# The first two pairs' modulation fetched pair by pair, and three small loads written later

## The chip, the cores and the metric

The kernel runs on one core of one Trainium2 chip. The metric is the device time of one execution in microseconds (us). A core has five engines, each with its own in-order instruction queue, that meet only at semaphores: TensorE (PE in the profile, its weight loads PEld), VectorE (DVE), ScalarE (ACT), GpSimd (POOL) and SyncE (SP). In this kernel SP does nothing but issue DMAs. Sixteen DMA engines move what SP and POOL issue.

## The reference

One layer over 256 latent tokens `x` and 256 context tokens `ctx`, width 2048, all in float32. Only the beginning matters here:

```python
mod_x = (silu(c)     @ w_mod + b_mod).reshape(1, 1, 9, 2048)   # w_mod: 2048 x 18432
mod_c = (silu(c_ctx) @ w_mod + b_mod).reshape(1, 1, 9, 2048)
# first half-step feed-forward, the same for x (mod_x) and ctx (mod_c):
h = rms_norm(x, norm_ffn1) * (1 + mod[1]) + mod[0]
x = x + 0.5 * mod[2] * ((silu(h @ w_gate) * (h @ w_up)) @ w_down)   # 2048 -> 5504 -> 2048
# then: mixer (gated heads | two-direction scan), second feed-forward, final norm
```

So the first feed-forward can't start before parts 0 and 1 of `w_mod` (2 x 2048 columns, 33.5 MB) have been read, multiplied and applied, at least for the input channels it starts with. The scan heads have three small parameter rows, `dt_bias`, `a_log` and `d_skip`, used much later.

## The kernel before, in words

The 2048 channels are 16 tiles of 128, taken as eight **pairs** (kp = 0 to 7). Both token sets stand side by side, 512 columns. Every product is done in three matmuls (`mm3`, L116 to L118): each float32 operand is cut into a high part `hi` (ACT, L68) and a rest `lo` (DVE, L69), and hi*hi, hi*lo and lo*hi are added up.

Start: SP loads x and ctx (tiles `xin`), PE transposes them (L296), ACT squares them, DVE and POOL add the squares up. `rstd_rows` makes the row norm from that: `total` (16 small matmuls, L272), `root` (DVE, ACT, DVE up to `dg`), `spread` (a matmul, L283, and the ACT copy `R`).

Modulation of pairs (`first_mods`, L529): `w_mod` comes in 512 KB tiles `raw`, which are multiplied on PE with silu(c) (`sc`). Eight tiles make up one pair's share of parts 0 and 1, sixteen that of two pairs. A **half** is the work on two tiles: four matmuls of 512 columns, or eight of 256. With `cnt` = 2, two pairs are done together, first all of part 1, then all of part 0, from tiles of 128 x 2 x 512, so with rows of 2 KB in memory. With `cnt` = 1, one pair has both parts in one bank, from tiles of 128 x 4 x 256, rows of 1 KB. After the last half of a bank DVE copies it out (`m`, L373), PE turns it (L378), DVE reduces it and adds the bias (L381, L386), and `scale_of` (L393) makes the scale from part 1. `first_h(kp)` then makes the pair's input: DVE multiplies by the row norm (`xr`, L324), ACT applies scale and shift (`hh` and `t`, L332), DVE takes the rest (`hl`, L337).

First feed-forward columns (`first_cols`): for each pair, gate and up weights of 3 x 128 columns (two tiles of 384 KB, called g0, u0 for pair 0 and so on), 36 matmuls of 512 columns for each pair, into six banks. This is a loop over pairs, 288 matmuls in all, and between them the halves of later pairs are woven in at numbered places (`weave`, the table `between`; a place is one mm3, and pair kp begins at place 12*kp). After it come five chunks of the feed-forward, whose weights no longer need a modulation first.

Order: each engine's queue is fixed when the program is built. A scheduler places the instructions by priorities of its own; the order in which the code is written, and the places of `weave`, steer it, and only the pinned instructions (`keep_in_program_order`) keep their written order. SP's queue is in order too, so a load that waits for a buffer holds up all loads behind it. All weight tiles share one pool of seven buffers `raw` (`rp`, bufs=7); a tile is loaded once its buffer's former tile has been used: by PE for `w_mod`, by ACT and DVE for weights that are cut into hi and lo. The cut halves share three buffers each.

Of the kernel before, what the change touches and what calls it, by code (L numbers as in the profile page):

```python
# [15 lines left out]
P = 128  # L16
# [18 lines left out]
def tile_block(ctx: ExitStack, tc: tile.TileContext, a, out: bass.AP):  # L35
# [18 lines left out]
    def const(shape, n, dt=F32):  # L54
        return cp.tile(shape, dt, tag=n, name=n)

    def small(t, src):
        nc.gpsimd.dma_start(t, src)

    def raw(shape, src):  # L60
        t = rp.tile(shape, F32, tag="raw", name=uid("raw"))
        nc.sync.dma_start(t, src)
        return t
# [14 lines left out]
    def loaded(shape, src):  # L78
        return lambda: split(raw(shape, src), shape)
# [29 lines left out]
    def mbank():  # L109
        return mp.tile([P, 512], F32, tag="mi", name=uid("mi"))  # L110
# [18 lines left out]


    bias_bc = const([P, 32], "bias_bc")
    small(bias_bc, a["dt_bias"].rearrange("o d h -> o (d h)").partition_broadcast(P))
    alog_bc = const([P, 32], "alog_bc")
    small(alog_bc, a["a_log"].rearrange("o d h -> o (d h)").partition_broadcast(P))
    dsk = const([P, NH], "dsk")
    small(dsk, a["d_skip"].partition_broadcast(P))


    cv = const([P, 2, KT], "cv")
# [65 lines left out]
    def then(f):  # L205
        tasks[-1][2].append(f)
# [42 lines left out]
    def xcol(k, v):  # L249
        return xpair(k // 2, v)[:, k % 2, :]  # L250
# [116 lines left out]
    def mod_take(ps, parts):  # L367

        st = {}

        def copy():
            st["m"] = slot([P, 512], n="m")
            tc.keep_in_program_order(nc.vector.tensor_copy(st["m"], ps))  # L373

        def turn():
            pt = mbank()
            for i in range(4):
                nc.tensor.transpose(pt[:, i * P:(i + 1) * P], st["m"][:, i * P:(i + 1) * P], ident)  # L378
            for i, (part, tp) in enumerate(parts):
                dst = MOD[part][:, 2 * tp:2 * tp + 2, :]  # L380
                nc.vector.tensor_reduce(  # L381
                    out=dst,
                    in_=pt[:, i * 256:(i + 1) * 256].rearrange("p (t g w) -> p t w g", g=4, w=32)[:, :, 0:2, :],
                    axis=mybir.AxisListType.X, op=ALU.add,
                )
                tt(dst, dst, bmod(part, 2 * tp, 2).unsqueeze(2).broadcast_to([P, 2, 2]), op=ALU.add)  # L386

        return copy, turn

    def scale_of(part, n, k0=0, k1=KT):  # L390

        m = MOD[part][:, k0:k1, :]
        stt(m, m, 1.0, vec(n, k0, k1 - k0).unsqueeze(2).broadcast_to([P, k1 - k0, m.shape[2]]),  # L393
            op0=ALU.add, op1=ALU.mult)

    def column(part):
        return lambda k, v: MOD[part][:, k, v:v + 1]
# [99 lines left out]
    def first_mods(k0, cnt):  # L497


        steps, turns = [], []  # L500

        def bank_of(parts):
            st = {}

            def half(i, j0):

                w = []
                part, kp = parts[i]
                n0 = part * D + kp * 256

                def load():
                    for x in range(2):
                        if cnt == 2:
                            w.append(raw([P, 2, 512], wmod[:, j0 + 2 * x:j0 + 2 * x + 2, n0:n0 + 512]))
                        else:
                            w.append(raw([P, 4, 256], wmod[:, j0 + 4 * x:j0 + 4 * x + 4, n0:n0 + 256]))

                first, last = ((0, 1, 2, 3), (12, 13, 14, 15)) if cnt == 2 else ((4, 5, 6, 7), (8, 9, 10, 11))

                def run_():  # L520
                    if not st:
                        st["ps"] = mbank()
                        st["take"] = mod_take(st["ps"], parts)

                    for y in ((2, 3, 0, 1) if cnt == 2 else (4, 5, 6, 7, 0, 1, 2, 3)):
                        j, g = j0 + y, y % 4
                        o, src = (st["ps"], w[y // 2][:, y % 2, :]) if cnt == 2 else (
                            st["ps"][:, i * 256:(i + 1) * 256], w[y // 4][:, g, :])
                        tc.keep_in_program_order(nc.tensor.matmul(  # L529
                            o[32 * g:32 * g + 32, :], lhsT=sc[:, j, :], rhs=src, start=(j == first[g]), stop=(j == last[g])))  # L530

                return load, run_

            if cnt == 2:
                steps.extend(half(0, j0) for j0 in range(0, KT, 4))
            else:
                steps.extend(half(i, j0) for i in range(2) for j0 in range(0, KT, 8))
            steps.append((None, lambda: st["take"][0]()))
            turns.append(lambda: st["take"][1]())

        if cnt == 2:
            for part in (1, 0):
                bank_of(((part, k0), (part, k0 + 1)))
        else:
            bank_of(((1, k0), (0, k0)))
        turns.append(lambda: scale_of(1, "norm_ffn1", 2 * k0, 2 * (k0 + cnt)))
        return steps, turns
# [3 lines left out]
    def first_h(kp):  # L551
        for _, f in modulated(kp, (0, 1), lambda v: R0["R"][:, v * TX:(v + 1) * TX], column(1), column(0)):
            f()

    m0, t0 = first_mods(0, 2)
    for load, _ in m0:
        if load:
            load()
    total, root, spread = [f for _, f in pieces]
    for f in (*[f for _, f in m0[:5]], total, small_turn, root, *[f for _, f in m0[5:7]], t0[0], spread,  # L560
              *[f for _, f in m0[7:]], *t0[1:], lambda: first_h(0)):
        f()

    between = {1: [lambda: first_h(1)]}
    later = []

    def place(at, f):
        between.setdefault(at, []).append(f)  # L570

    def weave(k0, cnt, at):
        steps, turns = first_mods(k0, cnt)
        for (load, f), x in zip(steps, at):
            if load:
                later.append(load)
            place(x, f)
            if load:
                place(x, ahead)
        place(at[len(steps)], lambda: [t() for t in turns])  # L580
        place(at[len(steps)], lambda: first_h(k0))
        if cnt == 2:
            place(12 * k0 + 1, lambda: first_h(k0 + 1))
# [2 lines left out]
        if later:  # L586
            later.pop(0)()

    weave(2, 2, [1, 3, 5, 7, 8, 9, 11, 13, 15, 16, 17])
    weave(4, 2, [19, 21, 24, 26, 27, 29, 32, 34, 37, 38, 39])  # L590
    weave(6, 1, [42, 46, 50, 54, 55, 56])
    weave(7, 1, [58, 62, 66, 70, 71, 73])

    g0 = []

# [53 lines left out]
    def down(m0, n, act_t, vs, after=lambda dg: None, steps=1, budget=0.0):  # L649
        a0, a1 = vs[0] * TX, (vs[-1] + 1) * TX  # L650

        def fold(d, ps):
            while len(gates_done) <= d // 8:
                next(bg)
            for v in vs:
                x = xcol(d, v)
                stt(x, ps[:, v * TX:(v + 1) * TX], MOD[2][:, d, v:v + 1], x, op0=ALU.mult, op1=ALU.add)

        def unit(dg, st, f0, fn):
            def mm(hl_):  # L660
                hi, lo = hl_
                if f0 == 0:
                    st.extend([(dbank if dg % 2 else bank)() for _ in range(2)])
                for dd in range(2):
                    c = slice(dd * P, (dd + 1) * P)
                    for i in range(fn):
                        f = f0 + i
                        h, l = act_t[f]
                        mm3(st[dd][:, a0:a1], (hi[:, i, c], lo[:, i, c]), (h[:, a0:a1], l[:, a0:a1]), f == 0, f == n - 1)

            add(loaded([P, fn, 256], krows(wd, m0 + f0, fn, dg * 256, 256)), mm, steps, budget)

        for dg in range(KP):
            st = []
            for f0 in range(0, n, 4):
                unit(dg, st, f0, min(4, n - f0))
            for dd in range(2):
                then(lambda dg=dg, dd=dd, st=st: fold(2 * dg + dd, st[dd]))
            then(lambda dg=dg: after(dg))
# [22 lines left out]
    for ci, n in enumerate(chunks):  # L702
        m0 = m
        act_t = []
        if m == 0:
            for t in range(N0):
                then(lambda t=t, dst=act_t: gated(dst, g0[t], g0[N0 + t]))
            m = N0
        while m < m0 + n:
            pair(m, act_t, 1.5 if ci == 0 else 1.2)  # L710
            m += 2
        if ci < len(chunks) - 1:
            down(m0, n, act_t, (0, 1), steps=0.9 if ci == 0 else 0.7)
    then(lambda: [None for _ in bg])
    then(root_table)
    for v in range(2):
# [694 lines left out]
    t0 = len(tasks) - 8  # L1411
# [108 lines left out]
```

## Time and profile before

| | |
|---|---|
| median of 3 runs | 2655.83 us (2655.7 to 2657.45) |
| the profiled execution | 2657.01 us, its span 2655.3 us |
| PE busy | 2616.2 us, 99% of the span |
| DVE, ACT, POOL busy | 1617.7, 979.6, 56.2 us |
| HBM read | 492.77 MB, 186 GB/s over the span |

The profile is one execution on the chip. Busy time is given by engine and by stretch of time; a wait is put down to the instruction or DMA whose semaphore came last. The granted clock is the share of TensorE's full speed; 1.00 is the level of 2.4 GHz and 0.50 that of 1.2 GHz, and a stretch with both has a value in between.

### The profile page before, as it was taken

To read this page: it belongs to the slowest core of one execution; us is meant where nothing else is said; L and a number is where in the kernel's file an instruction comes from. 1 tells how busy PE (TensorE), PEld (TensorE's weight loads), DVE (VectorE), ACT (ScalarE), POOL (GpSimd) and SP (SyncE) were. 2 spreads that over 40 slices of the span, in tenths; PEclk is the share of its full clock that TensorE was granted. 3 is DMA by queue.
4 is the path that set the end of the run, shared out by engine and by line. 5 is a ranking of instruction groups with operands and counts; after the bars stand their busy time and mean duration, and the time that the engine had idled before them with its cause. 6 is when DMAs were issued, how large, how long until landed. Compare 5 with 4: busy or idle time off the path is not lost.

```text
span 2655.3 us, 31810 instructions
## 1 busy us (share of the span) xinstructions
PE 2616.2 (99%) x12309; PEld 2132.3 (80%) x12309; DVE 1617.7 (61%) x2167; ACT 979.6 (37%) x1326; POOL 56.2 (2%) x84
## 2 busy tenths in 40 slices
PE   6999999999999999999999999999999999999998
PEld 3577888888888888888889977778788888888896
DVE  3378987876555556556324855876654445455646
ACT  4342222212222222222223654765564443434344
POOL 2000000000000000000000000021010000000000
PEclk8999999999999999999999999999999999999999
DMA  9976766657665766766434543355666666666664
GB/s 314 317 240 201 224 211 203 195 172 211 203 194 164 217 189 207 220 190 205 119 102 132 175 131 88 111 173 164 199 199 189 192 189 194 188 195 186 196 179 139
DMA packets 333547, 499.06 MB, mean 188 GB/s; under 512 B 18835, under 2 KB 169683, under 8 KB 333395
## 3 DMA queue, kind: packets, MB, share of 16 engines
q1 hardware_dynamic: 331059, 491.21, 60.0%
q0 software_dynamic: 2336, 5.81, 0.9%
q8 instruction: 96, 1.57, 0.2%
q14 instruction: 56, 0.46, 0.0%
HBM read 492.77 MB, written 2.10 MB: 186 GB/s over the span
## 4 chain that ended last, share of the span: by engine, by line
PE 95%; DMA 2%; DVE 1%; ACT 1%; issue 0%; SPq 0%; ACTq 0%; DVEq 0%
PE gu L116 25%; PE gu L117 25%; PE gu L118 25%; PE dn L116 5%; PE dn L117 5%; PE dn L118 5%; PE mi L529 1%; DMA raw<-in_w_mod_dram 1%; PE dn L982 0%; DVE cy L903 0%; PE mi L411 0%; PE mi L1356 0%; PE mi L1052 0%; PE mi L1081 0%; ACT hi L68 0%
## 5 line engine op out<-in xcount | busy, mean ns | idle before, releaser
L69 DVE TENSOR_TENSOR lo<-raw,hi 128x1024 fp32r<-128x1024 f32 (+1 forms) x634 | 759.9, 1199 | 777.8 <-ACT hi L68 777.0
L68 ACT CAST hi<-raw 128x1024 fp32r<-128x1024 f32 (+1 forms) x634 | 650.1, 1026 | 1446.0 <-PE gu L117 755.5
L116 PE MATMUL gu<-hh,hi 128*128 128x512 f32 x1504 | 590.0, 393 | 1.9 <-ACT hh L332 1.6
L118 PE MATMUL gu<-hh,lo 128*128 128x512 f32 x1504 | 587.2, 390 | 0.0
L117 PE MATMUL gu<-hl,hi 128*128 128x512 f32 x1504 | 587.1, 390 | 0.0
L459 DVE SCALAR_TENSOR_TENSOR macc<-raw,sc,macc 128x512 f32<-128x512 f32 x600 | 424.5, 746 | 4.9
L116 PEld LDWEIGHTS gu<-hh,hi 128*128 128x128 f32 x1504 | 283.0, 188 | 75.5 <-issue 7.2
L116 PE MATMUL gu<-hi,hh 128*128 128x512 f32 (+1 forms) x864 | 336.3, 390 | 0.0
L117 PE MATMUL gu<-lo,hh 128*128 128x512 f32 (+1 forms) x864 | 334.3, 387 | 0.0
L118 PE MATMUL gu<-hi,hl 128*128 128x512 f32 (+1 forms) x864 | 333.6, 386 | 0.0
L117 PEld LDWEIGHTS gu<-hl,hi 128*128 128x128 f32 x1504 | 282.9, 188 | 61.2 <-issue 4.3
L118 PEld LDWEIGHTS gu<-hh,lo 128*128 128x128 f32 x1504 | 282.6, 188 | 61.3 <-issue 2.2
L116 PEld LDWEIGHTS gu<-hi,hh 128*128 128x128 f32 x864 | 162.3, 188 | 32.0 <-issue 1.4
L117 PEld LDWEIGHTS gu<-lo,hh 128*128 128x128 f32 x864 | 162.3, 188 | 31.8 <-issue 1.4
L118 PEld LDWEIGHTS gu<-hi,hl 128*128 128x128 f32 x864 | 162.2, 188 | 31.8 <-issue 0.7
L116 PE MATMUL gu<-ah,hi 128*128 128x512 f32 (+1 forms) x408 | 145.6, 357 | 0.0
L116 PE MATMUL dn<-ah,hi 128*128 128x512 f32 (+1 forms) x408 | 145.4, 356 | 0.0
L118 PE MATMUL dn<-ah,lo 128*128 128x512 f32 (+1 forms) x408 | 145.4, 356 | 0.0
L117 PE MATMUL dn<-al,hi 128*128 128x512 f32 (+1 forms) x408 | 145.2, 356 | 0.0
L117 PE MATMUL gu<-al,hi 128*128 128x512 f32 (+1 forms) x408 | 145.2, 356 | 0.0
L118 PE MATMUL gu<-ah,lo 128*128 128x512 f32 (+1 forms) x408 | 145.1, 356 | 0.0
L116 PEld LDWEIGHTS dn<-ah,hi 128*128 128x128 f32 x408 | 77.1, 189 | 12.6 <-ACT hi L68 0.8
(309 smaller groups left out, 2549.4 us busy)
## 6 DMA issues: line engine op xcount, KB each, us to landing
raw<-in_w_mod_dram SPq DMA_DIRECT2D x288, 512.0 KB, 4.7
raw<-in_ffn_w_down_dram SPq DMA_DIRECT2D x172, 512.0 KB, 3.9
raw<-in_ffn_w_gate_dram SPq DMA_DIRECT2D x160, 512.0 KB, 4.4
raw<-in_ffn_w_up_dram SPq DMA_DIRECT2D x160, 512.0 KB, 4.2
raw<-in_w_in_dram SPq DMA_DIRECT2D x72, 512.0 KB, 3.7
raw<-in_w_out_dram SPq DMA_DIRECT2D x32, 512.0 KB, 3.8
raw<-in_ffn_w_gate_dram SPq DMA_DIRECT2D x16, 384.0 KB, 4.0
raw<-in_ffn_w_up_dram SPq DMA_DIRECT2D x16, 384.0 KB, 3.4
```

Source lines behind the costliest of these rows:

```text
L68: a = nc.scalar.copy(hi, src)
L69: b = nc.vector.tensor_tensor(lo, src, hi.bitcast(F32), op=ALU.subtract)
L116: nc.tensor.matmul(ps, lhsT=wh, rhs=xh, start=first, stop=False)
L117: nc.tensor.matmul(ps, lhsT=wh, rhs=xl, start=False, stop=False)
L118: nc.tensor.matmul(ps, lhsT=wl, rhs=xh, start=False, stop=last)
L459: tc.keep_in_program_order(stt(acc[v], w[:, i, :], s, acc[v], op0=ALU.mult, op1=ALU.add))
L529: tc.keep_in_program_order(nc.tensor.matmul(o[32 * g:32 * g + 32, :], lhsT=sc[:, j, :], rhs=src, start=(j == first[g]), stop=(j == last[g])))
```

## The change

The first two pairs are no longer done together. Pair 0 alone is fetched and done ahead of the column loop (eight tiles of 128 x 4 x 256 in place of sixteen of 128 x 2 x 512). Pair 1 is woven into pair 0's columns (`weave(1, 1, ...)`), and the places of the later pairs are moved. In the start, `small_turn`, `total` and `root` are written among the four halves of pair 0, and the turn after the copy. The three loads of the heads' parameters are written behind the second feed-forward chunk.

```diff
-    small(bias_bc, a["dt_bias"]...)      # and a_log, d_skip
+    def head_parameters():
+        small(bias_bc, a["dt_bias"]...)  # and a_log, d_skip
...
-    m0, t0 = first_mods(0, 2)
+    m0, t0 = first_mods(0, 1)
...
-    for f in (*[f for _, f in m0[:5]], total, small_turn, root, *[f for _, f in m0[5:7]], t0[0], spread,
-              *[f for _, f in m0[7:]], *t0[1:], lambda: first_h(0)):
+    for f in (*[f for _, f in m0[:2]], total, small_turn, root, m0[2][1], spread, m0[3][1], m0[4][1], *t0, lambda: first_h(0)):
...
-    between = {1: [lambda: first_h(1)]}
+    between = {}
...
-    weave(2, 2, [1, 3, 5, 7, 8, 9, 11, 13, 15, 16, 17])
-    weave(4, 2, [19, 21, 24, 26, 27, 29, 32, 34, 37, 38, 39])
+    weave(1, 1, [1, 3, 5, 7, 8, 10])
+    weave(2, 2, [9, 11, 12, 13, 14, 15, 16, 17, 18, 19, 22])
+    weave(4, 2, [24, 26, 28, 30, 31, 32, 34, 36, 38, 39, 42])
...
+        if ci == 1:
+            then(head_parameters)
```

From the end of the first columns on, every engine's queue is the same as before. Up to there the same instructions stand in another order, with four more small ones on DVE. On POOL the scheduler puts the three loads at the start again, only behind the first masks instead of ahead of `ident`.

**First place, VectorE (DVE) at the step from pair 0 to pair 1.** Before, pair 1's scale and shift came with pair 0's, and its `xr` and `hl` follow pair 0's; `lo_180` is u1's rest, and `m_183` the first copy of pairs 2 and 3:

```order
L337 TENSOR_TENSOR hl_73_323<-t_133_476,hh_72_322 128x512
L324 TENSOR_TENSOR xr_167_544<-xt_23_151,R_127_445 128x512
L69 TENSOR_TENSOR lo_154_517<-raw_152_514,hi_153_516 128x768
L324 TENSOR_TENSOR xr_168_546<-xc_31_159,R_127_445 128x512
L337 TENSOR_TENSOR hl_75_325<-t_169_548,hh_74_324 128x512
L337 TENSOR_TENSOR hl_77_327<-t_170_553,hh_76_326 128x512
L69 TENSOR_TENSOR lo_180_600<-raw_178_597,hi_179_599 128x768
L373 COPY m_183_620<-mi_171_560 128x512
```

Now, with `lo_165` as u1's rest and `m_168` as the copy of pair 1's modulation:

```order
L339 TENSOR_TENSOR hl_73_320<-t_122_445,hh_72_319 128x512
L69 TENSOR_TENSOR lo_165_565<-raw_163_562,hi_164_564 128x768
L375 COPY m_168_589<-mi_156_513 128x512
L326 TENSOR_TENSOR xr_173_616<-xt_23_148,R_116_414 128x512
L326 TENSOR_TENSOR xr_174_618<-xc_31_156,R_116_414 128x512
L383 TENSOR_REDUCE mod1_308<-mi_172_606 128x4
```

The copy that pair 1's input hangs on now stands behind the rest of u1, a tile that before pair 1's input did not wait for.

**Second place, SyncE (SP) ahead of pair 2.** The `raw` tiles in the order of their issue. Before, from u1 (`raw_178`) to g2 (`raw_189`), the tile whose rest DVE takes ahead of the last copy for pairs 2 and 3:

```order
L62 DMA raw_178_597<-in_ffn1_w_up_dram 128x2x384
L62 DMA raw_181_613<-in_w_mod_dram 128x2x512
L62 DMA raw_182_615<-in_w_mod_dram 128x2x512
L62 DMA raw_185_630<-in_w_mod_dram 128x2x512
L62 DMA raw_186_632<-in_w_mod_dram 128x2x512
L62 DMA raw_187_644<-in_w_mod_dram 128x2x512
L62 DMA raw_188_646<-in_w_mod_dram 128x2x512
L62 DMA raw_189_648<-in_ffn1_w_gate_dram 128x2x384
```

Now, from g2 (`raw_179`) to u2 (`raw_194`); here it is u2 whose rest (`lo_196`) DVE takes ahead of the last copy (`m_199`):

```order
L62 DMA raw_179_643<-in_ffn1_w_gate_dram 128x2x384
L62 DMA raw_182_656<-in_w_mod_dram 128x2x512
L62 DMA raw_183_658<-in_w_mod_dram 128x2x512
L62 DMA raw_184_667<-in_w_mod_dram 128x2x512
L62 DMA raw_185_669<-in_w_mod_dram 128x2x512
L62 DMA raw_188_684<-in_w_mod_dram 128x2x512
L62 DMA raw_189_686<-in_w_mod_dram 128x2x512
L62 DMA raw_190_695<-in_w_mod_dram 128x2x512
L62 DMA raw_191_697<-in_w_mod_dram 128x2x512
L62 DMA raw_192_706<-in_w_mod_dram 128x2x512
L62 DMA raw_193_708<-in_w_mod_dram 128x2x512
L62 DMA raw_194_710<-in_ffn1_w_up_dram 128x2x384
```

By the semaphores in the built programs g2 took the buffer of u1 before (free when DVE has cut u1), and u2 now takes the buffer of `raw_184` (free when PE has run the seventh half of pairs 2 and 3, `raw_185` and `raw_184`).

**Third place, TensorE (PE) at the step from pair 1 to pair 2.** Before, from the eighth half of pairs 2 and 3 over the last turn to pair 2's first matmul:

```order
L529 MATMUL mi_184_625<-raw_186_632,sc_135 32x512 x2
L529 MATMUL mi_184_625<-raw_185_630,sc_135 32x512 x2
L378 MATMUL mi_198_699<-ident_128,m_196_685 128x128 x4
L529 MATMUL mi_206_737<-raw_188_646,sc_135 32x512 x2
L529 MATMUL mi_206_737<-raw_187_644,sc_135 32x512 x2
L529 MATMUL mi_206_737<-raw_193_666,sc_135 32x512 x2
L529 MATMUL mi_206_737<-raw_192_664,sc_135 32x512 x2
L116 MATMUL gu_155_520<-hh_78_328,hi_190_650 128x512
```

Now, from the seventh half on:

```order
L531 MATMUL mi_187_679<-raw_185_669,sc_132 32x512 x2
L531 MATMUL mi_187_679<-raw_184_667,sc_132 32x512 x2
L117 MATMUL dn_148_493<-hl_77_324,hi_164_564 128x512
L118 MATMUL dn_148_493<-hh_76_323,lo_165_565 128x512
L380 MATMUL mi_200_741<-ident_125,m_186_674 128x128 x4
L116 MATMUL dn_149_494<-hh_76_323,hi_164_564 128x512
L117 MATMUL dn_149_494<-hl_77_324,hi_164_564 128x512
L118 MATMUL dn_149_494<-hh_76_323,lo_165_565 128x512
L531 MATMUL mi_187_679<-raw_189_686,sc_132 32x512 x2
L531 MATMUL mi_187_679<-raw_188_684,sc_132 32x512 x2
L380 MATMUL mi_201_750<-ident_125,m_199_730 128x128 x4
L116 MATMUL gu_144_489<-hh_78_325,hi_180_645 128x512
```

Before, two halves of pairs 4 and 5 stand between the last turn and pair 2's first matmul; now nothing does.

## Rows read from the trace of the kernel before

**Rows 1.** Stretches: length, busy us of five engines, granted clock, DMA share, GB/s.
```profile
83.29:152.50 69.21, 64.94 (x389) 42.41 (x386) 30.15 (x57) 33.67 (x58) 0.00 (x0) 0.97 0.92 309
21.00:42.00 21.00, 15.70 (x89) 5.13 (x89) 7.38 (x19) 6.77 (x11) 4.78 (x4) 0.76 1.05 389
118.50:128.00 9.50, 9.50 (x62) 6.82 (x51) 3.67 (x5) 4.90 (x9) 0.00 (x0) 1.00 1.08 357
```

**Rows 2.** Timeline of PE ahead of the columns: start, us, instruction [idle before <-releaser].
```profile
24.63 1.93 PE L529 MATMUL mi<-raw,sc 128*32 128x512 f32 x8 [1.57 <-DMA raw<-in_w_mod_dram]
...
33.96 1.95 PE L272 MATMUL dn<-ones,sq 128*128 128x1 f32 x16
...
37.41 1.12 PE L283 MATMUL dn<-dg,ones 128*128 128x512 f32 x2
...
43.56 1.94 PE L529 MATMUL mi<-raw,sc 128*32 128x512 f32 x8 [1.66 <-DMA raw<-in_w_mod_dram]
...
49.03 2.07 PE L116 MATMUL gu<-hh,hi 128*128 128x512 f32 x4 [1.59 <-ACT hh L332]
```

**Rows 3.** Timeline of PE in the columns: halves, two matmuls, turns.
```profile
53.59 1.15 PE L529 MATMUL mi<-raw,sc 128*32 128x512 f32 x8
...
67.83 0.39 PE L117 MATMUL gu<-hl,hi 128*128 128x512 f32 x1
68.06 0.39 PE L118 MATMUL gu<-hh,lo 128*128 128x512 f32 x1
...
79.80 0.66 PE L378 MATMUL mi<-ident,m 128*128 128x128 f32 x4 [2.02 <-DVE m L373]
80.39 2.97 PE L529 MATMUL mi<-raw,sc 128*32 128x512 f32 x16
83.29 1.52 PE L116 MATMUL gu<-hh,hi 128*128 128x512 f32 x3
...
131.97 1.93 PE L529 MATMUL mi<-raw,sc 128*32 128x256 f32 x32
```

**Rows 4.** Timeline of ACT: cut of u1; cut of g2, input of pair 2; the same of pair 6.
```profile
67.89 0.83 ACT L68 CAST hi<-raw 128x768 fp32r<-128x768 f32 x1 [10.06 <-DMA raw<-in_ffn_w_up_dram]
77.32 0.83 ACT L68 CAST hi<-raw 128x768 fp32r<-128x768 f32 x1 [8.60 <-DMA raw<-in_ffn_w_gate_dram]
81.26 1.09 ACT L332 ACTIVATE hh<-xr,mod,mod 128x256 fp32r<-128x256 f32 x2 [3.11 <-DVE mod L386]
...
128.90 0.83 ACT L68 CAST hi<-raw 128x768 fp32r<-128x768 f32 x1 [3.23 <-DMA raw<-in_ffn_w_up_dram]
133.04 1.09 ACT L332 ACTIVATE hh<-xr,mod,mod 128x256 fp32r<-128x256 f32 x2 [3.31 <-DVE mod L393]
```

**Rows 5.** Timeline of DVE: rest of g2 and the copy behind it; the copy for pair 6.
```profile
78.19 0.96 DVE L69 TENSOR_TENSOR lo<-raw,hi 128x768 fp32r<-128x768 f32 x1 [4.18 <-ACT hi L68]
79.06 0.68 DVE L373 COPY m<-mi 128x512 f32<-128x512 f32 x1
...
130.64 0.68 DVE L373 COPY m<-mi 128x512 f32<-128x512 f32 x1
```

**Rows 6.** Timeline of SP: issue of u1 and of g2.
```profile
61.07 0.42 SPq L62 DMA_DIRECT2D raw<-in_ffn_w_up_dram  x1
...
71.83 0.42 SPq L62 DMA_DIRECT2D raw<-in_ffn_w_gate_dram  x1
```

**Rows 7.** The page, DMA issues: count, KB each, median us from issue to landing.
```profile
raw<-in_ffn_w_up_dram SPq DMA_DIRECT2D x16, 384.0 KB, 3.4
```

**Rows 8.** Timeline of ACT at the start: `a_log`'s exponential, the first square.
```profile
7.61 0.23 ACT L831 ACTIVATE alog_bc<-alog_bc 128x32 f32<-128x32 f32 x1 [5.52 <-DMA alog_bc<-in_a_log_dram]
...
9.87 0.63 ACT L301 ACTIVATE sq<-xt 128x512 f32<-128x512 f32 x1 [0.47 <-DVE xt L299]
```

**Rows 9.** Timeline of POOL at the start: first and last instruction now ahead of the loads.
```profile
3.07 0.22 POOL masks.py:197 MEMSET ident<- 128x128 f32 x1
...
4.42 0.29 POOL L181 TENSOR_SCALAR_AFFINE_SELECT GE<-ones 128x128 f32<-128x128 f32 x1
```

More of the change, by code (lines that the diff above doesn't have):

```diff
@@ L131, in tile_block @@
     bias_bc = const([P, 32], "bias_bc")
-    small(bias_bc, a["dt_bias"].rearrange("o d h -> o (d h)").partition_broadcast(P))
     alog_bc = const([P, 32], "alog_bc")
-    small(alog_bc, a["a_log"].rearrange("o d h -> o (d h)").partition_broadcast(P))
     dsk = const([P, NH], "dsk")
-    small(dsk, a["d_skip"].partition_broadcast(P))
+    def head_parameters():
+        small(bias_bc, a["dt_bias"].rearrange("o d h -> o (d h)").partition_broadcast(P))
+        small(alog_bc, a["a_log"].rearrange("o d h -> o (d h)").partition_broadcast(P))
+        small(dsk, a["d_skip"].partition_broadcast(P))
     cv = const([P, 2, KT], "cv")
@@ L587, in ahead @@
             later.pop(0)()
-    weave(2, 2, [1, 3, 5, 7, 8, 9, 11, 13, 15, 16, 17])
-    weave(4, 2, [19, 21, 24, 26, 27, 29, 32, 34, 37, 38, 39])
-    weave(6, 1, [42, 46, 50, 54, 55, 56])
-    weave(7, 1, [58, 62, 66, 70, 71, 73])
+    weave(1, 1, [1, 3, 5, 7, 8, 10])
+    weave(2, 2, [9, 11, 12, 13, 14, 15, 16, 17, 18, 19, 22])
+    weave(4, 2, [24, 26, 28, 30, 31, 32, 34, 36, 38, 39, 42])
+    weave(6, 1, [44, 47, 50, 53, 54, 57])
+    weave(7, 1, [59, 62, 65, 68, 69, 72])
     g0 = []
```

## The prediction

> **What bounds the kernel now.** I read the page first: PE is busy 99% of the span, so only the rest, and stretches at the lower clock, can be won or lost. Then the stretches. From 152.5 us on, the end of the first columns, every queue is unchanged, so a lead or a lag there is carried to the end; the change is decided in the first 152.5 us. Up to the first column matmul at 49.03 [rows 2] DMA sets the pace: 389 GB/s at full DMA share from 21 to 42 us, and PE waits for `raw` before its halves [rows 1, 2]. In the columns PE has the work of 69.2 us from pair 2 on and waits 69.21 - 64.94 = 4.3 us of it [rows 1]. The timelines say for what: at 79.80 a turn waits 2.02 us for the copy `m` [rows 3], and DVE makes that copy only after the rest of a weight tile that has just landed: g2's cut on ACT at 77.32, its rest at 78.19, the copy at 79.06, pair 2's input from 81.26 on [rows 4, 5]. So a pair starts when the weight tile ahead of its copy on DVE has landed. What a reader is to look for in the change is which tile that is, and when SP can issue it.
>
> **The start.** Eight tiles in place of sixteen come before the first turn. Two tiles land every (43.56 - 24.63) / 7 = 2.70 us [rows 2]. The new tiles have rows of 1 KB; a stretch in which most tiles are of that kind moved 357 GB/s against 389, both at full share [rows 1], so I take 2.70 x 389 / 357 = 2.95 us. The fourth two are there at 24.63 + 3 x 2.95 = 33.5, and g0, u0, g1 (0.393 MB, 1.1 us each) by 36.8. PE: the third half starts at 30.5 and ends at 32.5 (1.93 us); `total` takes 1.95 (to 34.4); from its end to `spread` 37.41 - 35.91 = 1.50 us pass; `spread` takes 1.12 (to 37.0), and behind it the fourth half, 1.1 (to 38.1) [rows 2]. DVE now has the rests of g0, u0 and g1 ahead of the copy: g1 is cut at 36.9, its rest starts 0.87 later, the copy 0.87 after that, at 38.7, by the two steps of [rows 5]. From a copy of one pair to the end of its first `hh` it was 133.04 + 1.09 - 130.64 = 3.49 us [rows 4, 5]. First column matmul: 42.2, with a little for the clock 42.5, against 49.03: **6.5 us sooner**.
>
> The page "DMA: Bandwidth & Descriptors" of the Trainium skill (Specifications) has transfers at line rate from 512 B on, by which rows of 1 KB would cost nothing; 357 against 389 GB/s speaks against it here. By the page the start would be 0.9 us sooner still.
>
> **Pair 1.** Its modulation is now done inside pair 0's columns, and its copy stands behind u1's rest on DVE (first place). SP issues u1 when the third half of pair 1 has run. From the first matmul to there: ten matmuls and a half at the lower clock, 53.59 + 1.1 - 49.03 = 5.6 us [rows 2, 3]; then eleven matmuls of 0.23 us (two in a row start at 67.83 and 68.06 [rows 3]) and two halves of 1.0 us, with 0.3 for the joints, 4.8. So 42.5 + 10.4 = 52.9, and u1 is issued 0.5 later, behind one more tile. How long it then takes has two rows: u1 before, 61.07 to its cut at 67.89, 6.8 us; g2, 71.83 to 77.32, 5.5 us [rows 4, 6]. Both had w_mod tiles queued in front, as u1 has now (three or four); I take 6.1, between them. The floor is 3.4 us, the page's median for such tiles later in the kernel [rows 7]. Cut at 59.5; from a cut to the end of the first `hh` it was 128.90 to 134.13, 5.23 us [rows 4]. Pair 1's first matmul: 64.7. PE has work for 15 matmuls, three halves and a turn of that, 7.1 us, and waits some 4.7.
>
> The same page (Anatomy of one DMA) gives one transfer as 2.0 us plus its bytes at 436 GB/s, so by estimate 2.9 us for 0.393 MB. The rows of 5.5 and 6.8 us are twice that, since four larger tiles share the engines; by the page the sum below would be smaller by twice 3.2 us, +3.2.
>
> **Pair 2.** SP issues u2 only when the seventh half of pairs 2 and 3 has run, and its rest stands ahead of the last copy (second place); before, it was g2, in the buffer of u1. Up to the end of that half PE has 31 matmuls (7.1 us) and five halves (5.0). A wait of 4 us or more before them puts the clock down: after the wait of 2.02 us at 79.80 two halves took 2.97 us and three matmuls 1.52, against 1.93 for as many columns at full clock and 0.7 to 0.9 [rows 3], so 1.6 us. End of the seventh half: 64.7 + 13.7 = 78.4; u2 issued at 78.9; cut at 85.0 by the same 6.1 us; first `hh` 82.35 - 77.32 = 5.03 us later [rows 4]. Pair 2's first matmul: 90.0, against 83.29 [rows 3]. Of the 11.6 us PE has work for 3.2 (five matmuls, the eighth half, two turns; third place).
>
> **The sum at pair 2.** 90.0 - 83.29 = +6.7. Before, two halves of pairs 4 and 5 were done by then, now not: +1.9. The lower clock after the long wait, 1.6, against 0.6 of it that lay behind 83.29 before: +1.0. Together **+9.6 us**. The waits behind pair 2 (4.3 us) I keep as they are: the copies of pairs 4 to 7 stand behind the rests of weight tiles as before. Against the profiled execution (2657.01) this is 2666.6; that one lies 1.2 above the median, so 2665.4, and I say **2665 us**.
>
> **What costs nothing.** The three head loads stay in the start, since the scheduler hoists them; they only move behind seven short POOL instructions, 3.07 to 4.71 [rows 9], so by 1.6 us. `a_log`'s exponential, now behind `sc` on ACT, moves from 7.61 to about 9.3 and ends before the first square at 9.87 [rows 8]; uncovered, it would push the squares by some tenths, and they have 5 us until `total`. On the DMA queues they move 40 KB. The four more DVE instructions are of 0.2 us each on an idle DVE. Work on PE and bytes are the same.
>
> **Ends of the unknown.** Landing between 3.4 and 6.8 us for each of the two tiles: -5.4 to +1.4. Start: -1 to +1. Waits behind pair 2: all 4.3 gone, or 2 to 3 more, since the two tiles held up make SP's later loads late too. All low ends together -1, all high ends +15; not all come at once, so 2658 to 2671 for the forecast itself.
>
> **Rivals.**
> 1. *The early start is carried through: faster.* For it: PE's work is the same and nothing behind 152.5 us changes, so 6.5 us sooner at the start is 6.5 at the end if no new wait comes. It decides at pair 1: u1 has to be cut so early that the turn waits for no more than the work in front of it, by 54.8, 1.4 us after its issue; the shortest row is 3.4. Only if SP issues u1 much earlier than I read. 2655.8 - 6.5 = 2649.
> 2. *DMA evens it out: no change.* The bytes up to a pair's start are nearly the same, and an idle queue lands tiles fast. With both landings at 3.4 us the sum is 9.6 - 5.4 = +4.2; with two thirds of the later waits of 4.3 gone, since the later places give PE more cover, +1: 2657. Against it: u2 is issued after the seventh half whatever the queue does.
> 3. *A larger loss.* The late halves of pairs 4 and 5 release their buffers late, and the copy of pair 4 waits again as pair 2's did, 3 to 5 us: 2669.
> 4. *The change does not do what it says.* For the head loads that is so (above), at no price; the modulation does move.
>
> **Chances.** Forecast (2660 to 2667) 50%, larger loss 20%, evened out 22%, carried through 8%. What a measurement of this kernel can tell from no change is about 0.2%, 5.3 us: faster is below 2650.5, slower above 2661.1. Faster 8%; within it nearly all of the second rival and a little of the forecast's low end, 25%; slower 67%. The range reaches down into the second rival, to 2653, and up over the third, to 2672.
>
> **What would show it.** In the new profile: the first column matmul near 42.5, PE waiting for `m` before the turn of pair 1 (some 62) and for 5 to 7 us before the last turn ahead of pair 2 (some 87 to 88), and ACT's cut of u2 just ahead, released by DMA; the end of the columns (the first Silu of the gate) some 10 us later than 152.5. Wrong would be: pair 2's first matmul by 84, or SP issuing u2 before the seventh half; then the sum fails at the buffer that I read for u2.

## The result and the profile after

After, the kernel takes 2673.61 us (median of 5 runs, 2672.16 to 2675.83), against 2655.83: 1.0064 times as long, 95% interval 1.0053 to 1.0076. The direction and the mechanism were forecast; the size was not: +17.8 us measured, +9.6 forecast, and the time lies above the range. The profiled run of after took 2672.16 us, so 15.2 more than that of before, and the profiles are compared on that.

First the two stretches before and behind the first column matmul, in before (split at 49.03) and in after (split at 45.63). The columns are those of [rows 1]: length, busy time of PE, PEld, DVE, ACT, POOL, granted clock, DMA share, GB/s.

```profile
0.00:49.03 49.03, 28.93 (x157) 13.80 (x157) 19.77 (x40) 19.82 (x32) 14.06 (x24) 0.84 0.94 318
49.03:165.00 115.97, 109.68 (x600) 69.70 (x601) 48.14 (x91) 51.56 (x87) 0.00 (x0) 0.95 0.87 293
```

```profile
0.00:45.63 45.63, 25.53 (x153) 15.86 (x153) 19.91 (x36) 20.23 (x33) 14.03 (x24) 0.81 0.86 270
45.63:165.00 119.37, 101.79 (x600) 59.27 (x601) 38.72 (x82) 41.21 (x74) 0.00 (x0) 0.92 0.86 293
```

Length minus PE busy is PE's idle time. Ahead of the columns it is 49.03 - 28.93 = 20.1 us before and 45.63 - 25.53 = 20.1 us after: the columns begin 3.4 us sooner, but PE has idled just as long; the halves not done by then must be done later. In the columns up to 165 us idle time goes from 6.3 to 17.6 us, +11.3. PE's busy time over the whole span goes from 2616.2 to 2620.4, +4.2. Together 15.5, and the spans differ by 15.2. So the loss is waiting in the columns, and a longer time for the same matmul columns: the granted clock there is 0.92 against 0.95, and at full clock a half takes 1.07 us in either form.

The start of after, on PE (start, us, instruction, idle before it and its releaser), answers to [rows 2]:

```profile
25.47 1.94 PE L531 MATMUL mi<-raw,sc 128*32 128x256 f32 x16 [1.05 <-DMA raw<-in_w_mod_dram]
...
31.41 1.93 PE L531 MATMUL mi<-raw,sc 128*32 128x256 f32 x16 [0.42 <-DMA raw<-in_w_mod_dram]
33.27 3.57 PE L274 MATMUL dn<-ones,sq 128*128 128x1 f32 x16
38.35 2.08 PE L285 MATMUL dn<-dg,ones 128*128 128x512 f32 x2 [1.51 <-DVE dg L281]
40.35 1.66 PE L531 MATMUL mi<-raw,sc 128*32 128x256 f32 x16
42.84 0.66 PE L380 MATMUL mi<-ident,m 128*128 128x128 f32 x4 [0.82 <-DVE m L375]
45.63 2.08 PE L116 MATMUL gu<-hh,hi 128*128 128x512 f32 x4 [2.14 <-ACT hh L334]
```

The tiles land in the rhythm that was forecast (halves 2.97 us apart), but `total` takes 3.57 us where [rows 2] had 1.95, and `spread` 2.08 where it had 1.12.

Then the two pairs. PE at the end of pair 1's third half, its turn and its first matmul, and from the seventh half of pairs 2 and 3 to pair 2's first matmul; these answer to [rows 3]:

```profile
55.93 1.07 PE L531 MATMUL mi<-raw,sc 128*32 128x256 f32 x16
...
65.20 0.66 PE L380 MATMUL mi<-ident,m 128*128 128x128 f32 x4 [1.14 <-DVE m L375]
68.00 1.36 PE L116 MATMUL gu<-hh,hi 128*128 128x512 f32 x4 [2.15 <-ACT hh L334]
...
71.00 1.69 PE L531 MATMUL mi<-raw,sc 128*32 128x512 f32 x8
...
81.73 1.07 PE L531 MATMUL mi<-raw,sc 128*32 128x512 f32 x8
...
84.52 1.07 PE L531 MATMUL mi<-raw,sc 128*32 128x512 f32 x8
93.92 1.12 PE L380 MATMUL mi<-ident,m 128*128 128x128 f32 x4 [8.33 <-DVE m L375]
96.62 2.07 PE L116 MATMUL gu<-hh,hi 128*128 128x512 f32 x4 [1.59 <-ACT hh L334]
```

The eighth half has ended at 85.6, and PE then waits 8.33 us for the copy `m`. ACT shows the cuts of u1 and u2 (answering to [rows 4]), DVE the rest of u2 and the copy behind it ([rows 5]):

```profile
62.72 0.83 ACT L68 CAST hi<-raw 128x768 fp32r<-128x768 f32 x1 [14.19 <-DMA raw<-in_ffn_w_up_dram]
...
91.44 0.83 ACT L68 CAST hi<-raw 128x768 fp32r<-128x768 f32 x1 [19.01 <-DMA raw<-in_ffn_w_up_dram]
```

```profile
92.31 0.96 DVE L69 TENSOR_TENSOR lo<-raw,hi 128x768 fp32r<-128x768 f32 x1 [7.72 <-ACT hi L68]
93.18 0.68 DVE L375 COPY m<-mi 128x512 f32<-128x512 f32 x1
```

DVE is free from 84.6 to 92.3 and the copy's input is there at 85.6; it stands behind the rest of u2, and u2 has not landed. SP issues it late, as [rows 6] had it for g2:

```profile
57.09 0.42 SPq L62 DMA_DIRECT2D raw<-in_ffn_w_up_dram  x1
...
72.73 10.46 SPq L62 DMA_DIRECT2D raw<-in_w_mod_dram  x10
83.28 0.42 SPq L62 DMA_DIRECT2D raw<-in_ffn_w_up_dram  x1
```

And the DMA over these stretches (columns as above):

```profile
70.60:74.00 3.40, 3.40 (x20) 0.66 (x18) 1.65 (x2) 1.14 (x2) 0.00 (x0) 0.75 0.18 31
74.00:91.40 17.40, 11.59 (x66) 5.59 (x62) 1.31 (x6) 0.00 (x0) 0.00 (x0) 0.94 1.01 364
```

From the end of the last half ahead of pair 1's turn to the end of the next half, at 72.7, PE frees no buffer, and the queue runs dry (31 GB/s). Then SP issues ten tiles of `w_mod` within 10.5 us, u2 behind them, and the queue runs at its full share until u2 is there.

Behind pair 2 nothing more is lost: from its first matmul to the first Silu (168.00, before 152.54) PE's idle time is 71.38 - 67.00 = 4.4 us, against 4.3 in [rows 1]:

```profile
96.62:168.00 71.38, 67.00 (x401) 42.69 (x402) 29.15 (x56) 33.60 (x59) 0.00 (x0) 0.98 0.87 293
```

### The profile page after: what moved, and what is told of

Same layout as the page of the kernel before. It is cut to its first block, busy times and chain, and to the rows that moved or that the text cites. A ratio compares the mean times of both kernels' runs of the same rounds, so it can differ in the third digit from the quotient of the medians.

```text
span 2670.5 us, 31939 instructions
## 1 busy us (share of the span) xinstructions
PE 2620.4 (98%) x12373; PEld 2136.7 (80%) x12373; DVE 1617.8 (61%) x2168; ACT 979.0 (37%) x1326; POOL 56.0 (2%) x84
## 4 chain that ended last, share of the span: by engine, by line
PE 93%; DMA 3%; DVE 2%; ACT 1%; issue 0%; SPq 0%; ACTq 0%; DVEq 0%
PE gu L116 25%; PE gu L117 25%; PE gu L118 25%; PE dn L116 5%; PE dn L117 5%; PE dn L118 5%; DMA raw<-in_ffn_w_up_dram 1%; PE mi L531 1%; DMA raw<-in_w_mod_dram 1%; DMA raw<-in_ffn_w_gate_dram 0%; PE dn L986 0%; DVE cy L907 0%; PE mi L413 0%; PE mi L1360 0%; ACT hi L68 0%
```

## The experiments

The theory A that they test: a pair's copy `m` stands, in DVE's fixed order, behind the rest of a weight tile that lands late; moving pair 1's modulation into the columns makes that tile later. The main rivals: the bytes ahead of a pair's start set the pace (B), or another part of the change does it (C). Every ratio is to the kernel before, run on the same chip beside it, with a 95% interval. The diffs are shortened: `...` and the comments stand for what is left out.

**heads_only.** Before, with only the three head loads moved.

```diff
-    small(bias_bc, ...); small(alog_bc, ...); small(dsk, ...)
+    def head_parameters(): ...      # and then(head_parameters) behind the second chunk
```

> The kernel before with one part of the change alone: the three head loads written behind the second feed-forward chunk (the scheduler still puts them at the start, behind the first masks). Theory A (the loss is two waits for weight tiles that stand ahead of a pair's copy on DVE): this part has no share, 2655.8 +- 2 us. Rival C (part of the loss of 17.8 us comes from the start, where a_log's exponential now stands between sc and the squares on ACT): slower by 1 us or more, the first square later than 9.9 us.

2657.01 us, ratio 1.0001 (0.9993 to 1.001), and the first square starts at 9.72 us. This part of the change costs nothing that can be told.

**cut_late_2** and **cut_late.** After, with u2 (in cut_late u1 too) loaded at the same place in SP's queue, but cut only behind the copy.

```diff
+    cut_behind(8, 1, 1)       # u1, in cut_late only: split() written at place 8
+    cut_behind(19, 2, 1)      # u2: split() written at place 19
-        add(loaded(...), mm)
+        add(load only, mm)    # for these tiles
```

> The changed kernel, with u2 loaded at the same place of SP's queue, but cut into hi and rest behind the last copy of pairs 2 and 3, so that DVE has that copy ahead of u2's rest. Theory A: the turn ahead of pair 2 follows the eighth half (near 86.5 instead of 93.9) and pair 2's first matmul comes near 89 instead of 96.6; the kernel is 6 to 7 us faster than the changed one, 2666 to 2668 us. Rival B (DMA sets it: the bytes for pairs 2 and 3 and their weights are there no sooner, and PE waits for u2 a few matmuls later): within 1.5 us of the changed kernel, 2672 to 2675.

> As the one before, and the same for u1 and pair 1's copy. Theory A: the copy of pair 1 comes right behind its fourth half (near 59.5 instead of 64.5), but its turn stands behind two halves of pairs 2 and 3 on PE (to 64.1), so only 1 to 2 us more are won: 2664 to 2667 us. Rival B: no further gain.

cut_late_2 took 2668.68 us (1.0045, 1.0032 to 1.0058), just above theory A's range. Its last turn (86.89) and pair 2's first matmul (89.50) came where A had them, 7.1 us sooner than in after, but its span is only 4.3 us shorter. Cut_late took 2663.94 (1.003, 1.0017 to 1.0042). Cut_late on PE: pair 1's first matmul, pair 2's last turn and first matmul.

```profile
65.51 1.21 PE L116 MATMUL gu<-hh,hi 128*128 128x512 f32 x4 [0.82 <-ACT hh L334]
...
83.91 0.66 PE L380 MATMUL mi<-ident,m 128*128 128x128 f32 x4 [0.91 <-DVE m L375]
86.51 1.65 PE L116 MATMUL gu<-hh,hi 128*128 128x512 f32 x3 [1.95 <-ACT hh L334]
```

The bytes and SP's order are those of after, and pair 2 starts 10.1 us sooner. By the ratios 0.34%, some 9 us, of the loss was waiting behind the rests of u1 and u2. This is theory A's share, and B can't have it. What is left is 0.3%; by the table below, 3.2 us more waits in the columns than in before and 4.2 us more busy time of PE.

**u2_ahead.** After, with DVE's order kept, u2's rest ahead of the copy, and one load moved on SP: u2 goes ahead of the four `w_mod` tiles of pairs 4 and 5 that stood in front of it. (Its numbers are read from the second feed-forward's up matrix, the same rows, shape and bytes.)

```diff
+    eighth = later.pop()
+    def with_u2():
+        eighth()
+        fetched[2, 1] = raw(shape, krows(wu, 4, 2, 0, N0 * P))
+    later.append(with_u2)
```

> The kernel after, with one load moved on SyncE: u2 is issued ahead of the first four w_mod tiles of pairs 4 and 5, behind which it stood. VectorE's order is the same, u2's rest still stands ahead of the last copy for pairs 2 and 3. After, SyncE issued ten w_mod tiles from 72.7 to 83.2 us and then u2, whose cut came at 91.4. Theory A (u2 lands late because the tiles in front of it are 5.2 MB, which the queue moves at 390 GB/s): with six tiles in front it is issued at 79, cut at 84 to 85, pair 2's first matmul at 89 to 91, the time 2666 to 2669. Rival B (u2's landing takes its 8 us from its issue, whatever stands in front): cut at 87, first matmul at 92.4, 2669 to 2671. Rival C (the four tiles moved behind are missed as much): halves of pairs 4 and 5 wait behind pair 2's start, 2672 to 2675.

2667.30 us (1.0046, 1.0034 to 1.0059). SP, then ACT, then PE:

```profile
73.27 4.90 SPq L62 DMA_DIRECT2D raw<-in_w_mod_dram  x6
78.22 0.87 SPq L62 DMA_DIRECT2D raw<-in_ffn_w_up_dram  x1
```

```profile
86.14 0.83 ACT L68 CAST hi<-raw 128x768 fp32r<-128x768 f32 x1 [12.92 <-DMA raw<-in_ffn_w_up_dram]
```

```profile
88.62 0.67 PE L380 MATMUL mi<-ident,m 128*128 128x128 f32 x4 [2.44 <-DVE m L375]
91.22 2.08 PE L116 MATMUL gu<-hh,hi 128*128 128x512 f32 x4 [1.94 <-ACT hh L334]
```

Issued 5.1 us sooner, cut 5.3 us sooner, pair 2's first matmul 5.4 us sooner, the time 0.18% lower by the ratios, 4.8 us: about one for one, as far as the intervals can tell. The time lies in theory A's range; cut and first matmul lie between A's (84 to 85, 89 to 91) and B's (87, 92.4). From issue to cut it is again 7.9 us, as B had it. But the queue in front of u2 was as long. The stretches from the first of the ten or six tiles to u2's issue, in after and in u2_ahead:

```profile
72.73:83.28 10.55, 10.55 (x57) 4.96 (x58) 1.38 (x2) 0.00 (x0) 0.00 (x0) 1.00 0.90 305
73.27:78.22 4.95, 4.95 (x27) 2.23 (x28) 1.64 (x2) 0.00 (x0) 0.00 (x0) 1.00 0.76 236
```

By estimate the queue had moved 3.2 of the 5.2 MB issued in the one and 1.2 of 3.1 MB in the other, so that about 2 MB, four tiles, stood in front of u2 both times. At the 364 GB/s that after's queue moved from 74.00 to 91.40 that is 5.5 us. So this run shows that the place of the load counts, and it does not separate a backlog (A) from a fixed time (B).

**warm_start** and **cut_late_warm.** Four transposes of a constant ahead of each half of pair 0, in after and in cut_late.

```diff
+                    if cnt == 1 and k0 == 0:
+                        dummy = bank()
+                        for _ in range(4):
+                            tc.keep_in_program_order(nc.tensor.transpose(dummy[:, 0:P], ident, ident))
```

> The kernel after, with four transposes of a constant (results unused) ahead of each of the four halves of pair 0's modulation. After, TensorE ran the halves of the start, the sum of squares (3.57 us) and the spread (2.08 us) at the level of 1.2 GHz, and the first column matmul came at 45.6 where 42.5 was forecast. Theory A (the clock cost the 3.1 us, because TensorE is idle between the halves of the start): the sum takes about 2.0 us, the spread 1.1, the first column matmul comes at 42.5 to 43.5, and the time is 2670 to 2671.5, since pairs 1 and 2 keep their waits and pass on what comes before them. Rival B (DMA sets the pace up to there, the weight tiles land no sooner): first column matmul at 45 to 46 and a time of 2673 to 2674, whatever the clock does.

> The same four transposes ahead of each half, in the kernel cut_late (2663.9 us, u1 and u2 cut only behind the copies), which still was 7 us slower than before though no long wait for a weight tile was left. Theory A (of these 7 us about 3 are the lower clock of the start, the rest the waits of pair 1's serial steps): first column matmul 42.5 to 43.5, time 2660 to 2661.5. Rival B (the queue of tiles in front of pair 1 and 2 takes back what the start wins): first column matmul sooner by up to 3 us, but the first matmuls of pairs 1 and 2 where they were in cut_late, 65.5 and 86.5, and a time of 2663 to 2664.

Warm_start: 2671.66 us (1.006, 1.0047 to 1.0072). Two stretches of it, and PE from `spread` to pair 2:

```profile
21.00:34.00 13.00, 8.82 (x89) 5.59 (x87) 6.00 (x12) 6.03 (x10) 5.56 (x4) 1.00 1.08 355
34.00:42.00 8.00, 3.96 (x32) 1.93 (x26) 6.08 (x13) 3.14 (x5) 0.00 (x0) 0.89 0.96 310
```

```profile
35.23 1.12 PE L285 MATMUL dn<-dg,ones 128*128 128x512 f32 x2 [0.95 <-DVE dg L281]
...
43.22 2.07 PE L116 MATMUL gu<-hh,hi 128*128 128x512 f32 x4 [1.79 <-ACT hh L334]
...
94.94 2.07 PE L116 MATMUL gu<-hh,hi 128*128 128x512 f32 x4 [1.59 <-ACT hh L334]
```

The same two stretches of after:

```profile
21.00:34.00 13.00, 8.92 (x67) 4.11 (x66) 6.31 (x11) 6.43 (x10) 5.96 (x5) 0.64 1.09 353
34.00:42.00 8.00, 6.49 (x32) 3.85 (x31) 3.64 (x6) 2.98 (x5) 0.00 (x0) 0.53 0.87 283
```

The granted clock goes from 0.64 to 1.00 and from 0.53 to 0.89, each half takes 1.07 us in place of 1.93, and the columns begin 2.4 us sooner, as theory A had it. (Here the scheduler also ran the sum in two parts around the third half; the copy now stands behind the rests of g0, u0 and g1 on DVE, which end at 39.6, and no longer behind PE.) The medians of the two kernels differ by 1.9 us, less than the intervals can tell, and the time lies between A's and B's; the profiled spans differ by 2.0. Cut_late_warm took 2662.48 us (1.002, 1.0011 to 1.0029), 1.5 under cut_late, which the intervals can't tell from nothing either: between the two expectations. In its profile the clock fell again (0.57 from 34 to 42 us), and the columns began at 44.67, only 1.1 us sooner.

**old_places** and **late_places.** After with the old places of pairs 4 to 7, and before with the new ones.

```diff
-    weave(4, 2, [24, 26, 28, 30, 31, 32, 34, 36, 38, 39, 42])   # and 6, 7
+    weave(4, 2, [19, 21, 24, 26, 27, 29, 32, 34, 37, 38, 39])   # old_places; late_places the other way
```

> The kernel after with the places of pairs 4 to 7 as they were before (19 to 39, 42 to 56, 58 to 73), so that only the first three pairs' places are changed. Theory A (the loss is made ahead of pair 2's first matmul; the later places only decide about waits of about 1 us each): 2671 to 2675, pair 2's first matmul at 96 to 98 as after, perhaps a little later, since four more halves stand ahead of it. Rival C (the later places, with the halves of pairs 4 to 7 pushed towards their use, cost the rest of what cut_late still lacks): 2667 or less.

> The kernel before with one part of the change alone: the places of pairs 4 to 7 are those of the kernel after (24 to 42, 44 to 57, 59 to 72). Theory A (these places only move waits of about 1 to 2 us around): 2654 to 2659, no difference that can be told. Rival C (they push the halves towards their use, and the copies wait longer): 2661 or more. The kernel after with the old places came out 2 us faster than after, so from 0 to 2 us slower than before is what the two runs would have in common.

2671.45 us (1.0053, 1.0041 to 1.0066) and 2660.20 (1.0013, 1.0005 to 1.0022). Put into before, the later places cost 3.2 us, a little more than theory A gave them; taken out of after, they give back 2.2, which the intervals can't tell from nothing. So at most they have a small share, of two to three microseconds. In old_places the long wait is spread: PE's longest wait for `m` is 1.6 us, but just ahead of pair 2 three halves wait 3.7 us together for `w_mod` tiles, and pair 2's first matmul is at 97.78.

**two_three_ones.** After, with pairs 2 and 3 one by one, so with half the `w_mod` tiles ahead of pair 2.

```diff
-    weave(2, 2, [9, 11, 12, 13, 14, 15, 16, 17, 18, 19, 22])
+    weave(2, 1, [11, 13, 15, 17, 18, 20])
+    weave(3, 1, [21, 23, 25, 27, 28, 31])
```

> The kernel after, with pairs 2 and 3 also done one by one (pair 2 at places 11 to 20, pair 3 at 21 to 31), so that eight w_mod tiles in place of sixteen must be read before pair 2 can start, though in rows of 1 KB. The rest of u2 stays ahead of pair 2's copy on VectorE. Theory A (what counts is when u2 lands): with fewer tiles in front of u2 it is issued some 5 us sooner, pair 2's first matmul comes at 90 to 93, but pair 3's copy then waits in its turn, and the time is 2667 to 2673. Rival B (what counts is the amount of data ahead of pair 2): eight tiles less are 4.2 MB, at 300 GB/s 14 us of DMA time, pair 2 waits for nothing, its first matmul comes at 84 to 86, and the time is 2656 to 2662.

2676.98 us (1.0074, 1.0062 to 1.0087): above both ranges.

```profile
65.46 0.66 PE L380 MATMUL mi<-ident,m 128*128 128x128 f32 x4 [4.33 <-DVE m L375]
...
89.59 1.12 PE L380 MATMUL mi<-ident,m 128*128 128x128 f32 x4 [6.94 <-DVE m L375]
...
94.01 1.20 PE L116 MATMUL gu<-hh,hi 128*128 128x512 f32 x4
```

Eight tiles fewer ahead of pair 2, and it still waits 6.94 us for `m` behind the rest of u2 (cut at 87.11), and pair 1's turn now waits 4.33, with fewer halves to fill its time (its first matmul, at 68.26, is hardly later). Rival B is out: with 4.2 MB less in front, pair 2 starts 2.6 us sooner, and not 11 to 13. Theory A's own numbers missed too (pair 2 at 94.0, not 90 to 93): it had not counted that two halves of the next pair stand between the turn and that matmul.

**both_first.** After, with pair 1's modulation ahead of the columns again, but pair by pair, in rows of 1 KB, and the old places.

```diff
+    m1, t1 = first_mods(1, 1)      # loaded with m0, run ahead of the columns
-    weave(1, 1, [1, 3, 5, 7, 8, 10])
-    weave(2, 2, [9, 11, 12, 13, 14, 15, 16, 17, 18, 19, 22])
+    weave(2, 2, [1, 3, 5, 7, 8, 9, 11, 13, 15, 16, 17])
```

> The kernel after, with pair 1's modulation also done ahead of the columns, pair by pair, in rows of 1 KB, and the places of all later pairs as before. So the start is fetched in 16 tiles again, and nothing of pair 1 is woven into the columns. Theory A (the loss is made by pair 1's modulation in the columns, which takes cover and time from pairs 1 and 2): first column matmul at 51 (16 tiles at 357 in place of 389 GB/s, 49.0 before), pair 2's first matmul at 85 to 86, time 2657 to 2660. Rival B (pair by pair, with rows of 1 KB and a copy for each pair, loses by itself): 2665 or more.

2662.35 us (1.002, 1.0011 to 1.003), between the two expectations; the columns begin at 53.88, not 51. PE's idle time is near that of before (19.7 ahead of the columns, 7.8 from there to 165 us), but its busy time is 2622.2, +6.0. Of that, 5.3 us lie ahead of the columns, where PE is busy for 34.2 us with the same work (sixteen tiles) and not for 28.9, at a lower clock. In its stretch from 34 to 42 us the queue, too, moves less; there before had a granted clock of 1.00 and moved 384 GB/s:

```profile
34.00:42.00 8.00, 5.68 (x28) 2.75 (x27) 1.72 (x4) 0.79 (x2) 0.00 (x0) 0.50 0.77 235
```

The clock alone isn't it: heads_only had 0.54 in that stretch, 342 GB/s, and its columns began at 48.83. So the start of both_first, taken whole, costs 0.2%, some 5 us. Between it and after lie 0.44%: weaving pair 1 in and the new places. How much of the 0.2% is in after, whose start has half as many tiles, isn't shown.

**before_cut** and **before_cut_8.** The lesson put into before: g2, g4 and u5 loaded as before, but cut behind the copies that stood behind them. Before_cut_8 has eight buffers `raw` and two slots less; but it differs in one thing more, which its expectation doesn't name: the three tiles are also loaded only where they are cut.

```diff
+    cut_behind(16, 2, 0)
+    cut_behind(38, 4, 0)
+    cut_behind(55, 5, 1)
-    rp = ... bufs=7          # before_cut_8: bufs=8, NSLOT 70 -> 68, load written with the cut
```

> The kernel before with the same edit at its own three places where a copy stands behind a rest: g2 and pairs 2 and 3, g4 and pairs 4 and 5, u5 and pair 6. Theory A: of its waits of 2.02, 2.27 and 1.13 us for these copies and the lower clock behind the first two, 3 to 5 us go: 2651 to 2653 us. Rival B: the waits come back as waits for the same tiles or for w_mod, 2655 to 2657 us.

> The kernel before_cut (2652.4 us: before, with g2, g4 and u5 cut only behind the copies that stood behind them), with eight buffers for raw tiles in place of seven, paid for by two slots less. Theory A (the loads come one tile, 0.52 MB, earlier each time, and what PE still waits for in the columns, 3.1 us for cut weights and 3.9 for w_mod tiles, shrinks by half): 2649 to 2651. Rival B (these waits follow from the order on ACT and from the DMA rate at the start, not from buffers): 2652 to 2653. Rival C (two slots less hold up later stages): 2655 or more.

Before_cut: 2652.38 us, ratio 0.9984 (0.9976 to 0.9993), in theory A's range. It is faster than both kernels. The turn of [rows 3] that waited 2.02 us now waits 0.91, and pair 2 waits for the cut of g2 instead:

```profile
77.58 0.66 PE L378 MATMUL mi<-ident,m 128*128 128x128 f32 x4 [0.91 <-DVE m L373]
...
81.39 0.96 PE L116 MATMUL gu<-hh,hi 128*128 128x512 f32 x3 [2.16 <-ACT hi L68]
```

Before_cut_8 took 2662.74 us (1.0023, 1.0014 to 1.0033), which no expectation had:

```profile
89.12 0.79 PE L116 MATMUL gu<-hh,hi 128*128 128x512 f32 x1 [7.68 <-ACT hi L68]
```

```profile
78.11 0.37 SPq L62 DMA_DIRECT2D raw<-in_ffn_w_gate_dram  x1
```

There g2 is issued at 78.11 (70.73 in before_cut), its cut stands on ACT (88.26) behind pair 2's inputs and most of pair 3's, and PE waits 7.68 us for it. A cut can be too late as well as too early. Whether the buffer, the slots or the later load brought this about was not taken apart.

PE's account over the runs, by the views shown above for before and after (idle: length minus busy of the stretch):

| us | first column matmul | PE idle ahead of it | idle from there to 165 | PE busy, whole | span |
|---|---|---|---|---|---|
| before | 49.03 | 20.1 | 6.3 | 2616.2 | 2655.3 |
| after | 45.63 | 20.1 | 17.6 | 2620.4 | 2670.5 |
| warm_start | 43.22 | 19.3 | 17.4 | 2619.3 | 2668.5 |
| u2_ahead | 46.43 | 20.4 | 11.8 | 2620.7 | 2665.6 |
| cut_late | 45.79 | 20.0 | 9.5 | 2620.4 | 2662.5 |
| both_first | 53.88 | 19.7 | 7.8 | 2622.2 | 2662.2 |
| before_cut | 48.36 | 18.4 | 4.9 | 2616.4 | 2651.7 |

What is left of each span (12.1 to 12.7 us) is idle time behind 165 us, the same for all. The column "idle ahead" hardly moves with the start of the columns: a sooner start is no gain by itself. It moves by some 2 us without any change there (heads_only, with the start of before, has 17.5), so the 1.7 us that before_cut has less need not be its edit's; the 1.4 in the columns can be.

## Why the prediction was right and wrong

**The start** failed in its last terms. The rhythm of the tiles was right. But `total`, `spread` and the fourth half were taken at the durations of [rows 2], and now the three ran at the lower clock: 3.57 for 1.95, 2.08 for 1.12, 1.66 for 1.1, together 3.1 us, and the columns began at 45.63, not 42.5. Warm_start brings 2.4 of it back. [Rows 2] showed only one of two outcomes. In heads_only, whose start has PE's order of before, `total` stands behind the same halves with the same gap in front (0.78 us, 0.79 in before), and takes 3.58 us:

```profile
29.34 1.94 PE L531 MATMUL mi<-raw,sc 128*32 128x512 f32 x8 [0.78 <-DMA raw<-in_w_mod_dram]
...
32.06 1.94 PE L531 MATMUL mi<-raw,sc 128*32 128x512 f32 x8
33.92 3.58 PE L274 MATMUL dn<-ones,sq 128*128 128x1 f32 x16
```

So it isn't shown that the change brought the lower clock: in the profiles, kernels with the old start had 1.95 three times and 3.58 twice, kernels with the new one 1.95 once and 3.57 or 3.58 five times. There it cost nothing (columns at 48.83, 49.03 in before), since up to the columns DMA set the pace; after, the three stood in the chain to the first column matmul.

**Pair 1** was right but for that shift: issue at 57.1 (53.4 forecast), cut 5.6 us later (6.1), first matmul 5.3 us after the cut (5.2).

**Pair 2** was right in its mechanism: SP issued u2 right behind the seventh half, PE waited for the copy ahead of the last turn, and ACT's cut of u2, released by DMA, stood just in front. Its sizes were short. The seventh half ended at 82.8, 14.8 us after pair 1's first matmul (13.7 forecast, with nothing for the joints between halves and matmuls, for which pair 1's sum had 0.3). From issue to cut u2 took 8.2 us (6.1). By the Trainium skill, page "DMA: Bandwidth & Descriptors" (Anatomy of one DMA), the estimate was 2.9 us; the page gives its sum for one transfer, issued by GpSimd, and the trace differs: SP issued u2, and by the estimate at u2_ahead about four tiles stood in front of it. First matmul: 96.6 against 90.0.

**The sum at pair 2** stood at +9.6: +6.7, +1.9 for halves not yet done, +1.0 for the clock. The trace gives 96.62 - 83.29 = +13.3, and the stretch from there to the first Silu is 2.2 us longer than in [rows 1]: the halves, and little for the clock. The waits behind pair 2, kept at 4.3, are 4.4. So the mis-sized terms are three: the start (3.1 us), the seventh half (1.1) and u2's landing (2.1); with 0.3 from small steps they make 6.6 us at pair 2. What was added behind it came to 1.8 (15.2 - 13.3), not 2.9, so the profiled run lies 5.5 us above the sum. The median lies another 1.5 above the profiled run, the lowest of the five, where that of before lies 1.2 under its profiled run.

**What costs nothing** held (heads_only).

**The rivals.** "Carried through" was priced wrongly even for its own case: it held that 6.5 us sooner at the start are 6.5 at the end. PE idles 20.1 us ahead of the columns in both profiles, so beginning sooner only moves halves from where they fill PE's time beside the DMA to where they take column time; cut_late, without the long waits, is still 0.3% slower than before. "Evened out" fell with the measured time, and its ground, the bytes ahead of a pair, with two_three_ones. "A larger loss" came nearest in time (2669), but not by its cause: the copies of the later pairs waited no longer than before. The loss was the forecast's own wait, longer.

The loss of both_first comes with a lower clock and a slower queue in its start; which of pair by pair, the rows of 1 KB and the order of the small steps makes it was not taken apart.

## What to carry to other kernels

An engine's fixed order makes everything behind an instruction wait for that instruction's input: before a step is moved, look which late load stands in front of it on each engine, and put work that hangs on a load behind work whose input is there (before_cut gained 0.16% so, cut_late won back 0.34%). To start earlier is a gain only if the first engine idles less by it; add up its idle time ahead of the start before and after. A duration on TensorE that is taken from one profile holds at that profile's clock: give the sum at both levels, since the same sixteen small matmuls took 1.95 us in before and 3.58 in heads_only.

## What the hardware showed that was not expected

The queue of the `w_mod` tiles moves less with rows of 1 KB also in the start. From 21 to 34 us SP issues nothing else in both_first, with rows of 1 KB, and in before, with rows of 2 KB: 348 GB/s at a share of 1.07 in the first, 392 at 1.05 in the second:

```profile
21.00:34.00 13.00, 9.95 (x68) 5.21 (x68) 4.78 (x10) 5.98 (x9) 4.61 (x4) 0.55 1.07 348
21.00:34.00 13.00, 9.10 (x44) 2.12 (x44) 5.04 (x10) 5.98 (x9) 4.78 (x4) 0.61 1.05 392
```

With a few idle transposes, some 2.7 us of them in gaps in which PE waited anyway, the granted clock of the start was 1.00 in warm_start, where after had 0.64. It did not come out alike each time: with the same transposes cut_late_warm had 0.87 and then 0.57. As the clock of the start also differs between before and heads_only, one profile of each does not settle it; over the five executions of each, on two chips, the mean granted clock was 0.991 to 0.992 in after and 0.992 to 0.994 in warm_start.
